# A decoder step on one core: first two blocks of B together, then dt with both weight parts side by side

## The chip, the cores and the metric

The kernel runs on one core of one Trainium2 chip. The metric is device time in microseconds (us) of one execution. Engines are named as in the profile: PE multiplies matrices (PEld loads its stationary operand), DVE, ACT and POOL work on vectors, SP issues the DMAs.

## The reference, cut to what matters

One layer of a hybrid decoder. 304 tokens (16 meta, 256 of a prompt, 32 of eight running sequences) of width 2048 are normalized by RMSNorm and multiplied by one input projection, whose columns are the gate and input of an RG-LRU group, and z, x, B, C and dt of a Mamba-2 group. Convolution, recurrences, an output projection and a squared-ReLU MLP follow. For the change only this part matters:

```python
def rmsnorm(x, g):
    y = xf * lax.rsqrt(jnp.mean(xf * xf, axis=-1, keepdims=True) + EPS)
    return (y * g.astype(jnp.float32)).astype(x.dtype)
...
proj = h @ w_in            # h = rmsnorm(x, g_mix)
gate_lru, x_lru, z, xbc_raw, dt_raw = proj[..., :o1], ...
dt = jax.nn.softplus(dt_raw.astype(jnp.float32) + dt_bias.astype(jnp.float32))
```

dt has only 32 columns (one for each head). B and C have 512 columns each, x and z 2048 each, the LRU part 4096.

## The kernel before, in words

**Layout and tiling.** Features lie on the 128 partitions, tokens on the free axis. x is 16 tiles of 128 x 304 (index k). A *block* is 128 output columns of a projection: 16 k-tiles, and for each three matmuls, since float32 is multiplied as two parts: hi is the value rounded to the type that PE multiplies at full speed (fp32r), lo is the rest; the three products are hi·hi, weight hi times activation lo, weight lo times activation hi. So a block is 48 matmuls of some 304 columns into one PSUM bank (`gemm`, L92). The kernel has dt and 72 blocks of the input projection, 32 of the output projection, 64 and 64 of the MLP: 233 blocks.

**Weights.** `prep` (L74) loads a block's 1 MB into a raw buffer (two of these), ACT writes hi (L87) and DVE lo = raw − hi (L88) in two halves of eight k-tiles. There are four buffers for hi halves and four for lo halves, which hold two blocks. For the first blocks the 1 MB comes in four DMAs of 256 KB (`cuts`), later in one. `run_blocks` (L128) prepares up to two blocks ahead of the one that multiplies.

**Start.** SP issues, in this order, the dt weights (256 KB), the parameters (173 KB), 16 tiles of x (152 KB each), four quarters each of the first two blocks of B, the constants (380 KB) and a convolution state (288 KB). ACT writes hi of g_mix·x (x0h, L214), DVE lo (x0l, L215). POOL squares x tiles 0 to 7 (L218) and adds them in a tree (L220). The dt weights are copied four times across the 128 columns (L204), so that dt comes out on all four groups of 32 partitions; POOL makes the lo part of their second half (L207). dt is the first block, then B0 to B3, C0 to C3 and x tiles X0 to X3 (list ph1, L617), all on the x that is not yet normalized (x0): the scale 1/rms of a token is multiplied in when the block leaves PSUM (`rsb`). From X4 on the blocks use the normalized x (xa).

**What sets the order.** Work beside the matmuls is given out by generators. `pump` (L115) takes the next step of the first generator; it is called three times within a block and once behind it. The first generator is `norm_x` (L223): its first step emits the squares of tiles 8 to 15 (ACT) and their sums (DVE), then come seven empty steps, then the matmul that sums over partitions (`ms_all`, L170, the eighth pump), the square root, the reciprocal (L178), and the work of blocks that had to wait for the scale (`held`); from then on it normalizes one x tile in three pumps (L237 to L247), which fills xa. When it is through, `tables` (L335) makes dt's softplus and tables, and the SSD cores follow. Within these bounds the framework orders the instructions of each engine by a simulated timeline, earlier emission first; weight splits have a raised priority (L86). Engines then take their queues in order.

**PSUM.** There are eight banks: three take turns for blocks (pool psg), five for the rest and for the first three blocks (L94). A block's bank is free when its post step has read it; for B, C and X0 to X3 that is `fill_ext` (L280), which needs `rsb` and one of three `ext` buffers. So a block can begin once the post step of the third block before it has read its bank.

## Time and profile before

| what | us |
| --- | --- |
| time, median of 3 runs (least, greatest) | 1631.81 (1631.64, 1633.52) |
| the profiled execution's own time | 1631.34 |
| its span in the profile | 1629.2 |
| PE, PEld busy | 1606.7, 1579.8 |
| DVE, ACT, POOL busy | 1058.2, 831.3, 254.1 |

A busy PE is one that has a matmul in its pipeline; consecutive matmuls overlap, so their cost is read from the distance of their starts and not from their durations. "x0h", "whi" and so on are the program's names of tiles; "s" and "g" are PSUM banks of the two pools; L58, L61, L69 and L101 are lines of helpers that all tensor operations, fused operations, activations and block matmuls share, so tiles and shapes tell them apart.

### The profile page before, as it was taken

How to read it: one execution, taken by the hardware profiler on the slowest of the kernel's cores; microseconds unless marked ns; L12 is line 12 of the kernel's file. 1: busy time of each engine (PE TensorE's matmuls, PEld its weight loads, DVE VectorE, ACT ScalarE, POOL GpSimd, SP SyncE). 2: the span in 40 equal slices, each digit the busy share in tenths (PEclk: the TensorE clock that was granted, in tenths of full speed). 3: DMA queues.
4: the chain of work that ended last, by engine and by line, in shares of the span. 5: the costliest groups of instructions: out<-in, count | busy, mean ns of one | idle time of the engine just before them, and what ended most of it. 6: DMA issues, size and time to landing. Idle time of an engine off the chain costs nothing.

```text
span 1629.2 us, 28889 instructions
## 1 busy us (share of the span) xinstructions
PE 1606.7 (99%) x11855; PEld 1579.8 (97%) x11855; DVE 1058.2 (65%) x1542; ACT 831.3 (51%) x1299; POOL 254.1 (16%) x311
## 2 busy tenths in 40 slices
PE   7999999999999999999999999999999999999997
PEld 6999989889999999999999999999999999999997
DVE  7999998989787878456565434544445555455554
ACT  5656677557777774344444334443334433344442
POOL 4554534432232310011220000000000000000000
PEclk9999999999999999999999999999999999999999
DMA  6454555554444446454454444544544545445442
GB/s 218 156 181 148 196 194 196 174 188 151 164 166 165 166 151 225 158 176 158 156 176 161 160 177 156 168 168 158 175 160 160 176 156 170 167 158 175 160 162 104
DMA packets 53988, 274.28 MB, mean 168 GB/s; under 512 B 5984, under 2 KB 12768, under 8 KB 24544
## 3 DMA queue, kind: packets, MB, share of 16 engines
q1 hardware_dynamic: 53856, 272.44, 49.2%
q8 instruction: 93, 1.52, 0.4%
q14 instruction: 39, 0.32, 0.1%
HBM read 259.99 MB, written 12.42 MB: 167 GB/s over the span
## 4 chain that ended last, share of the span: by engine, by line
PE 92%; DMA 3%; DVE 2%; ACT 1%; issue 1%; POOL 0%; SPq 0%; DVEq 0%; POOLq 0%; ACTq 0%
PE g L101 86%; DMA out_sssd<-h 1%; PE s L101 1%; PE s L762 1%; DMA wraw<-in_win 1%; PE s L438 1%; DMA h<-in_stssd 1%; ACT whi L69 0%; POOL h0l L58 0%; DVE z L58 0%; PE s L562 0%; DVE h L58 0%; PE s L436 0%; PE s L559 0%; PE s L448 0%
## 5 line engine op out<-in xcount | busy, mean ns | idle before, releaser
L58 DVE TENSOR_TENSOR wlo<-wraw,whi 128x1024 fp32r<-128x1024 f32 (+1 forms) x470 | 572.7, 1221 | 428.7 <-ACT whi L69 425.1
L69 ACT ACTIVATE whi<-wraw 128x1024 fp32r<-128x1024 f32 (+1 forms) x470 | 491.6, 1048 | 649.2 <-PE g L101 593.2
L101 PE MATMUL g<-mh,whi 128*128 128x288 f32 x1024 | 303.5, 296 | 0.0
L101 PE MATMUL g<-hh,whi 128*128 128x288 f32 x1024 | 303.4, 296 | 0.0
L101 PE MATMUL g<-hl,whi 128*128 128x288 f32 x1024 | 302.8, 296 | 0.0
L101 PE MATMUL g<-ml,whi 128*128 128x288 f32 x1024 | 302.5, 295 | 0.0
L101 PE MATMUL g<-hh,wlo 128*128 128x288 f32 x1024 | 301.7, 295 | 0.0
L101 PE MATMUL g<-mh,wlo 128*128 128x288 f32 x1024 | 301.6, 295 | 0.0
L101 PE MATMUL g<-xh,whi 128*128 128x288 f32 (+1 forms) x960 | 287.8, 300 | 0.4 <-DVE ext L287 0.4
L101 PE MATMUL g<-xl,whi 128*128 128x288 f32 (+1 forms) x960 | 287.7, 300 | 0.0
L101 PE MATMUL g<-xh,wlo 128*128 128x288 f32 (+1 forms) x960 | 286.8, 299 | 0.0
L101 PEld LDWEIGHTS g<-hh,wlo 128*128 128x128 f32 x1024 | 193.1, 189 | 0.0
L101 PEld LDWEIGHTS g<-mh,wlo 128*128 128x128 f32 x1024 | 193.1, 189 | 0.0
L101 PEld LDWEIGHTS g<-hl,whi 128*128 128x128 f32 x1024 | 192.9, 188 | 0.0
L101 PEld LDWEIGHTS g<-hh,whi 128*128 128x128 f32 x1024 | 192.8, 188 | 0.0
L101 PEld LDWEIGHTS g<-ml,whi 128*128 128x128 f32 x1024 | 192.4, 188 | 0.0
L101 PEld LDWEIGHTS g<-mh,whi 128*128 128x128 f32 x1024 | 192.2, 188 | 0.0
L101 PEld LDWEIGHTS g<-xh,whi 128*128 128x128 f32 x960 | 180.7, 188 | 3.5 <-issue 1.0
L101 PEld LDWEIGHTS g<-xh,wlo 128*128 128x128 f32 x960 | 180.9, 188 | 2.7 <-issue 1.2
L101 PEld LDWEIGHTS g<-xl,whi 128*128 128x128 f32 x960 | 180.7, 188 | 2.2 <-issue 0.7
L101 PE MATMUL g<-lh,whi 128*128 128x288 f32 x256 | 75.8, 296 | 0.0
L101 PE MATMUL g<-sh,whi 128*128 128x288 f32 x256 | 75.8, 296 | 0.0
(273 smaller groups left out, 2329.3 us busy)
## 6 DMA issues: line engine op xcount, KB each, us to landing
wraw<-in_win SPq DMA_DIRECT2D x69, 1024.0 KB, 5.0
wraw<-in_wup SPq DMA_DIRECT2D x64, 1024.0 KB, 4.9
wraw<-in_wdn SPq DMA_DIRECT2D x64, 1024.0 KB, 4.9
wraw<-in_wout SPq DMA_DIRECT2D x32, 1024.0 KB, 5.0
h<-in_stssd SPq DMA_DIRECT2D x32, 256.0 KB, 3.1
out_sssd<-h SPq DMA_DIRECT2D x32, 256.0 KB, 3.0
wraw<-in_win SPq DMA_DIRECT2D x12, 256.0 KB, 5.1
big<-in_x SPq DMA_DIRECT2D x16, 152.0 KB, 3.5
```

The costliest lines, as they stand in the source:

```text
L58: e.tensor_tensor(out, a, b, op=op)
L69: A.activation(out, in_, f, **kw)
L101: TE.matmul(o, a[:, k % 8, :], b[:, c0:c1], start=n == 0, stop=n == 3 * NK - 1)
L438: TE.matmul(po[0:66, :], cm[:, 66 * b:66 * b + 66], a[:], start=b == 0 and n == 0, stop=b == 7 and n == 1)
L762: TE.matmul(pr[:, :FL], w_[:, m, :], x_[:], start=n == 0, stop=n == 2)
```

## The change

Where the tiles of x are loaded, the quarters of the weights of B0 and B1 are loaded and split in between (`take_w`, `split_w`), through one raw buffer of two halves. `run_first` multiplies B0 and B1 in one loop over k, six matmuls for each k-tile, and behind it dt: hi and lo of the 32 dt columns lie side by side in one stationary operand of 66 columns (two are zero), so dt takes two matmuls for each k-tile, 32 in place of 48; its two halves come out on partitions 0 to 31 and 32 to 63. `tables` adds them and spreads them over 128 partitions with one float32 matmul of 304 columns by a selection matrix, a step later than before. Eleven small matmuls on constants run at the start, before any data is there. The dt weights are loaded behind x. All 16 squares of x are ACT's, all sums are DVE's; POOL has none of them, nor a weight split. Normalizing a tile takes two pumps in place of three. `run_first` has one pump, so `ms_all` is emitted at the third pump within B3, and the held blocks are dt, B0, B1 and B2.

```diff
@@ -187,44 +187,88 @@
     rsb = x0p.tile([P, T], F32, tag="rsb", bufs=1, name="rsb")
     sqx = x0p.tile([P, 8, T], F32, tag="sqx", bufs=1, name="sqx")
     sqa = sqx[:, 0, :]
+    bf = [sp.tile([P, T], F32, tag="bf", bufs=4, name=f"bf{g}") for g in range(4)]
+    cf = [sp.tile([P, T], F32, tag="cf", bufs=4, name=f"cf{g}") for g in range(4)]
     held, scaled = [], []
     xts, x0, xa = [], [], []
     warm = cst.tile([P, 1], F32, name="warm")
     act(warm[:], ones[:], AF.Exp)
-    rdt = x0p.tile([P, NK, 32], F32, tag="rdt", bufs=1, name="rdt")
-    SY.dma_start(rdt[:], I["wdt"])
+    wps = bank()
+    for _ in range(11):
+        TE.matmul(wps[:, 0:P], ones[:].to_broadcast([P, P]), ones[:].to_broadcast([P, P]), start=True, stop=True)
     SY.dma_start(par[:], I["par"])
-    parts = []
+    first = [[], []]
+    raw4 = wp.tile([P, NK, P], F32, tag="wraw", bufs=2, name=nm("wraw"))
+    def take_w(q):
+        s0 = 8 * (q % 2)
+        for n, ap in enumerate(win[0:2]):
+            SY.dma_start(raw4[:, s0 + 4 * n:s0 + 4 * n + 4, :], ap[:, 4 * q:4 * q + 4, :])
+    def split_w(q):
+        s0, m = 8 * (q % 2), 4 * (q % 2)
+        for n, f in enumerate(first):
+            if m == 0:
+                f.append([wp.tile([P, 8, P], F32R, tag=t, bufs=4, name=nm(t)) for t in ("whi", "wlo")])
+            r = raw4[:, s0 + 4 * n:s0 + 4 * n + 4, :]
+            wh, wl = [t[:, m:m + 4, :] for t in f[-1]]
+            act(wh, r, AF.Copy)
+            tt(V, wl, r, wh.bitcast(F32), SUB)
     for k in range(NK):
-        if k % 8 == 0:
-            parts.append([wp.tile([P, 8, P], F32R, tag=t, bufs=4, name=nm(t)) for t in ("whi", "wlo")])
-        if k % 4 == 0:
-            r = rdt[:, k:k + 4, None, :].to_broadcast([P, 4, 4, 32])
-            wh, wl = [t[:, k % 8:k % 8 + 4, :].rearrange("p k (c j) -> p k c j", j=32) for t in parts[-1]]
-            act(wh, r, AF.Copy)
-            tt(V if k < 8 else G, wl, r, wh.bitcast(F32), SUB)
         xt = bigt()
         SY.dma_start(xt[:], I["x"][:, k, :])
         xts.append(xt)
+        if k % 4 == 1:
+            take_w(k // 4)
         gm = par[:, C_GMIX + k:C_GMIX + k + 1]
         hi = x0p.tile([P, T], F32R, tag="xh", name=nm("x0h"))
         lo = x0p.tile([P, T], F32R, tag="xl", name=nm("x0l"))
         act(hi[:], xt[:], AF.Copy, scale=gm)
         stt(lo[:], xt[:], gm, hi[:].bitcast(F32), MUL, SUB)
         x0.append((hi, lo))
-        if k < 8:
-            tt(G, sqx[:, k, :], xt[:], xt[:], MUL)
-    for n in (4, 2, 1):
-        tt(G, sqx[:, 0:n, :], sqx[:, 0:n, :], sqx[:, n:2 * n, :], ADD)
-    ready[id(wdt)] = parts
+        if k % 4 == 1:
+            split_w(k // 4)
+    rdt = x0p.tile([P, NK, 32], F32, tag="rdt", bufs=1, name="rdt")
+    SY.dma_start(rdt[:], I["wdt"])
+    wd = x0p.tile([P, 64 * NK + 2], F32R, tag="wd", bufs=1, name="wd")
+    wd3 = wd[:, 0:64 * NK].rearrange("p (k j) -> p k j", j=64)
+    V.memset(wd[:, 64 * NK:].bitcast(F32), 0.0)
+    act(wd3[:, :, 0:32], rdt[:], AF.Copy)
+    tt(V, wd3[:, :, 32:64], rdt[:], wd3[:, :, 0:32].bitcast(F32), SUB)
+    def run_first(posts):
+        pss_ = [bank() for _ in range(3)]
+        for k in range(NK):
+            for f, ps in zip(first, pss_[1:]):
+                hi, lo = f[k // 8]
+                xh, xl = x0[k]
+                for n, (a, b) in enumerate(((hi, xh), (hi, xl), (lo, xh))):
+                    TE.matmul(ps[:, :T], a[:, k % 8, :], b[:], start=k == 0 and n == 0,
+                              stop=k == NK - 1 and n == 2)
+        for k in range(NK):
+            for n, b in enumerate(x0[k]):
+                TE.matmul(pss_[0][0:66, :T], wd[:, 64 * k:64 * k + 66], b[:],
+                          start=k == 0 and n == 0, stop=k == NK - 1 and n == 1)
+        blocks[0] += 3
+        done.extend(range(3))
+        for ps, post in zip(pss_, posts):
+            held.append(lambda post=post, ps=ps: post(ps))
+        pump()
     def norm_x():
-        for k in range(8, NK):
-            sq = sp.tile([P, EXT], F32, tag="th", bufs=2, name=nm("sq"))
-            act(sq[:, :T], xts[k][:], AF.Square)
-            tt(V, sqa, sqa, sq[:, :T], ADD)
+        for k in range(NK):
+            act(sqx[:, k, :] if k < 8 else (bf + cf)[k - 8][:], xts[k][:], AF.Square)
+        for k in range(8):
+            tt(V, sqx[:, k, :], sqx[:, k, :], (bf + cf)[k][:], ADD)
+        for n in (4, 2, 1):
+            tt(V, sqx[:, 0:n, :], sqx[:, 0:n, :], sqx[:, n:2 * n, :], ADD)
         for _ in range(7):
             yield
         ms = ms_all(sqa, T)
@@ -242,7 +286,6 @@
             act(hi[:], xts[k][:], AF.Copy)
             tt(V, lo[:], xts[k][:], hi[:].bitcast(F32), SUB)
             xa.append((hi, lo))
-            yield
             yield
             yield
@@ -302,8 +345,6 @@
         return flat[:, S0:EXT].rearrange("p (b s) -> p b s", s=7)[:, :, 0:4]
-    bf = [sp.tile([P, T], F32, tag="bf", bufs=4, name=f"bf{g}") for g in range(4)]
-    cf = [sp.tile([P, T], F32, tag="cf", bufs=4, name=f"cf{g}") for g in range(4)]
     xf = [None] * 16
     yt_ = [None] * 16
     ys_ = []
@@ -329,14 +370,22 @@
     def post_dt(ps):
         x0 = bigt()
-        tt(V, x0[:], ps[:, :T], rsb[:], MUL)
+        tt(V, x0[0:64, :], ps[0:64, :T], rsb[0:64, :], MUL)
         gens.append(tables(x0))
-    def tables(x0):
+    def tables(y0):
+        yield
+        px = bank()
+        s4 = sp.tile([64, 4, 32], F32, tag="dup", bufs=1, name="s4")
+        V.tensor_copy(s4[:], con[0:64, None, K_SEL:K_SEL + 32].to_broadcast([64, 4, 32]))
+        TE.matmul(px[:, :T], flat(s4), y0[0:64, :],
+                  start=True, stop=True)
+        x0 = bigt()
+        V.tensor_scalar(x0[:], px[:, :T], par[:, C_DTB:C_DTB + 1], None, op0=ADD)
         b1, b2, b3 = [bigt() for _ in range(3)]
         dt = sp.tile([P, EXT], F32, tag="cv", bufs=2, name="dt")[:, :T]
         th1, th2 = [sp.tile([P, EXT], F32, tag="th", bufs=2, name=nm("th"))[:, :T] for _ in range(2)]
-        V.tensor_scalar(x0[:], x0[:], par[:, C_DTB:C_DTB + 1], None, op0=ADD)
         softplus(dt, x0[:], (b1[:], th1, th2, b2[:], b3[:]))
         nega = cst.tile([P, 1], F32, name="nega")
         act(nega[:], par[:, C_AL:C_AL + 1], AF.Exp)
@@ -609,19 +658,17 @@
                 gens.append(ssd_core(o // 4))
         return f
-    for w in win[0:2]:
-        ready[id(w)] = prep(w, 4)
-        done.append(id(w))
     SY.dma_start(con[:], I["con"])
     SY.dma_start(stsc[:], I["stsc"])
-    ph1 = [(wdt, x0, 0, T, post_dt)]
+    ph1 = []
     for g in range(4):
         ph1.append((win[g], x0, 0, T, lambda ps, g=g: post_conv(ps, 16 + g, bf[g], rsb)))
     for g in range(4):
         ph1.append((win[4 + g], x0, 12, T, lambda ps, g=g: post_conv(ps, 20 + g, cf[g], rsb, 12)))
     for o in range(4):
         ph1.append((win[8 + o], x0, 0, T, post_x(o)))
-    run_blocks(ph1, win[12:14])
+    run_first([post_dt] + [b[4] for b in ph1[:2]])
+    run_blocks(ph1[2:], win[12:14])
     while len(xa) < NK:
         pump()
     x0_stack.close()
```

## Rows read from the trace of the kernel before

**Rows 1.** The page, busy time, share of the span and instructions of each engine.
```profile
PE 1606.7 (99%) x11855; PEld 1579.8 (97%) x11855; DVE 1058.2 (65%) x1542; ACT 831.3 (51%) x1299; POOL 254.1 (16%) x311
```

**Rows 2.** PE's waits, whole span: us in total, times, longest.
```profile
PE s L101 <- ACT x0h L69: 6.2, 1, 6.2
PE s L101 <- DVE x0l L61: 3.2, 5, 1.8
...
PE g L101 <- DVE ext L287: 0.4, 1, 0.4
```

**Rows 3.** Timeline of PE: start us, duration us, line, operation, count.
```profile
22.06 0.46 PE L101 MATMUL s<-x0h,wlo 128*128 128x304 f32 x1
...
23.33 0.46 PE L101 MATMUL s<-x0l,whi 128*128 128x304 f32 x1
...
24.79 0.30 PE L101 MATMUL s<-x0l,whi 128*128 128x304 f32 x1
...
25.90 0.30 PE L101 MATMUL s<-x0h,whi 128*128 128x304 f32 x1
...
30.92 0.30 PE L101 MATMUL g<-x0h,whi 128*128 128x304 f32 x1
...
37.35 0.68 PE L173 MATMUL s<-sqx,ones 128*128 128x304 f32 x2
...
38.00 0.30 PE L101 MATMUL s<-x0l,whi 128*128 128x304 f32 x1
...
104.08 0.30 PE L101 MATMUL g<-xh,whi 128*128 128x304 f32 x1
```

**Rows 4.** Windows, block matmuls: stretch, length, PE busy (count), granted clock, DMA share, GB/s.
```profile
6.19:20.88 14.69, 11.45 (x34) 1.00 0.92 306
20.88:23.58 2.70, 2.70 (x11) 1.00 0.00 0
```

**Rows 5.** Groups of 0 to 24 us: shapes, count, busy us, mean ns, idle before.
```profile
L61 DVE SCALAR_TENSOR_TENSOR x0l<-big,par,x0h 128x304 fp32r<-128x304 f32 x16 | 16.4, 1100 | 0.3 <-ACT x0h L69 0.3
...
L58 POOL TENSOR_TENSOR sqx<-big 128x304 f32<-128x304 f32 x8 | 6.8, 875 | 4.7 <-DMA big<-in_x 4.7
...
L58 POOL TENSOR_TENSOR sqx<-sqx 128x1216 f32<-128x1216 f32 x1 | 2.9, 2877 | 0.1
```

**Rows 6.** Tile x0l, DVE: duration ns least, median, greatest; first and last start.
```profile
L61 DVE SCALAR_TENSOR_TENSOR x0l<-big,par,x0h x16: 523/960/3032, 6.2 to 22.1; 128x304 fp32r<-128x304 f32 x16
```

**Rows 7.** Timeline of SP's queue: DMAs issued.
```profile
0.74 0.39 SPq L197 DMA_DIRECT2D rdt<-in_wdt  x1
...
1.65 7.54 SPq L209 DMA_DIRECT2D big<-in_x  x16
9.23 3.98 SPq L78 DMA_DIRECT2D wraw<-in_win  x8
```

**Rows 8.** Timelines of POOL and ACT: first reader of three loads, which waited for it.
```profile
5.18 1.44 POOL L58 TENSOR_TENSOR sqx<-big 128x304 f32<-128x304 f32 x2 [4.75 <-DMA big<-in_x]
...
21.16 1.07 POOL L291 COPY ext<-stsc 128x24 f32<-128x24 f32 x3 [0.67 <-DMA stsc<-in_stsc]
...
13.85 0.63 ACT L69 ACTIVATE whi<-wraw 128x512 fp32r<-128x512 f32 x1 [0.33 <-DMA wraw<-in_win]
```

**Rows 9.** Tile cm, PE: matmuls with 66 stationary columns, duration ns least, median, greatest.
```profile
L438 PE MATMUL s<-h0h,cm x8: 390/396/403, 159.7 to 184.3; 128*66 128x512 f32 x8
```

**Rows 10.** Timeline of DVE: weight splits, the scale, the last xl, a bank's release.
```profile
22.54 4.90 DVE L58 TENSOR_TENSOR wlo<-wraw,whi 128x512 fp32r<-128x512 f32 x8
...
38.60 2.05 DVE L178 RECIPROCAL rsb<-rsb 128x304 f32<-128x304 f32 x1 [1.11 <-ACT rsb L69]
...
115.77 0.47 DVE L58 TENSOR_TENSOR xl<-big,xh 128x304 fp32r<-128x304 f32 x1
...
124.38 0.28 DVE L287 COPY ext<-g 128x32 f32<-128x32 f32 x2
```

**Rows 11.** Windows: length, then busy (count) of PE, PEld, DVE, ACT, POOL.
```profile
40.70:116.20 75.50, 75.50 (x551) 75.50 (x550) 71.28 (x146) 44.99 (x68) 38.35 (x47) 1.00 0.49 166
```

**Rows 12.** Groups of DVE, 41 to 116 us: shapes, count, busy us, mean ns.
```profile
L58 DVE TENSOR_TENSOR wlo<-wraw,whi 128x1024 fp32r<-128x1024 f32 x23 | 27.9, 1218 | 3.9 <-ACT whi L69 3.8
```

## Prediction

> **What bounds the kernel now.** I read the busy shares first, then PE's waits, then the first 40 us engine by engine, then the stretch from 40 to 125 us. PE is busy for 99% of the span [rows 1], and of its waits only the two at the start are long: 6.2 us until the first x0h, and five waits of 3.2 us together for x0l [rows 2]. So the kernel is PE's stream of matmuls from end to end, and what can be won is at the start, or matmuls left out.
>
> How fast PE runs is read from the distance of starts. At 22 us five matmuls take 1.27 us, 0.254 each, which is 304 columns at 1.2 GHz; from 24.79 to 25.90 eight take 1.11 us, 0.139 each, which is the 2.4 GHz level with some 0.012 us on top [rows 3]. The granted clock reads 1.00 in both stretches [rows 4], so only the distances show the level. PE ran at the lower one all through the dt block: from 6.19 to 20.88 us it was busy for 11.45 of 14.69 us, in pieces, and stayed low; from 20.88 to 23.58 it never stopped, and then rose [rows 4].
>
> B1 starts at 30.92 us [rows 3], so dt and B0 took until then, and the three blocks end 48 x 0.139 = 6.67 us later, at **37.6 us** (the matmul for the mean square, which cuts in at 37.35, left out). At full pace 144 matmuls are 20.0 us: the start loses 17.6 us.
>
> Why dt was slow stands in the DVE rows. The 16 x0l took 16.4 us, 1.10 us each [rows 5], while the shortest took 0.523 and the longest 3.03 us [rows 6]. The longest is as long as POOL's 1216-element sum, 2.88 us [rows 5]; POOL was squaring and adding all this time. So DVE's late x0l held PE, and DVE came to the weights of B0 only at 22.54 us [rows 10], though their first quarter was there at 13.85 [rows 8].
>
> **The change, part by part.** *Loads.* The first x tile was there at 5.18 us with 581 KB issued (dt weights, parameters, x0), the convolution state at 21.16 with all 5577 KB [rows 8]: 4996 KB in 15.98 us, 313 KB/us. The first weight quarter (3117 KB) fits to 0.4 us [rows 8]. The queue starts at 0.74 as before [rows 7]; the 256 KB of dt no longer stand in front, so x0 lands at 5.18 − 0.82 = 4.36, and what lies n KB into the queue at 4.36 + (n − 325)/313. In the new order: first quarters of B0, B1 (733, 989 KB) 5.7, 6.5; x5 (1597) 8.4; second quarters (2109) 10.1; x9 (2717) 12.0; third (3229) 13.6; x13 (3837) 15.6; fourth (4093, 4349) 16.4, 17.2; x15 (4653) 18.2; dt weights (4909) 19.0; B2 (6601) 24.4. SP takes 7.54/16 = 0.47 us for an x tile and 3.98/8 = 0.50 for a quarter [rows 7], 12 us in all, so the transfers and not SP set the pace. The third quarter's DMA waits for the first one's split, which stands ahead of x10; that split is through by about 8 us, when SP gets there, and the data in front lands until 12.0, so nothing runs dry.
>
> *Splits.* For four k-tiles DVE has four x0l of 0.52 us and two weight splits of 0.61 (4.90/8, [rows 10]): 3.3 us, against 1120 KB or 3.6 us of loads. This holds if x0l takes its short duration; since POOL has no sum or square left, I take that one. If x0l kept its mean of 1.10 us, four k-tiles would take 5.6 us, and the loop would end some 8 us later.
>
> *The loop.* B0's first matmul can start at 5.7 + 0.63 for hi [rows 8], 6.3 us, as early as dt's did. Six matmuls at 0.139 are 0.83 us for a k-tile, 13.3 us for the loop; at 0.254 they would be 1.52 us, more than the 0.9 us in which the data for one k-tile arrives. So a slow PE falls behind the loads, runs without a stop, and by [rows 4] rises; a fast one is held by the loads. The last quarters give whi and wlo at 17.0 to 18.5 us, and four k-tiles from 17.7 are through at 21.1. Behind it dt has 32 matmuls of 304 columns. With 66 stationary columns a matmul of 512 columns takes 0.39 to 0.40 us [rows 9], no less than its columns need, so I take 0.139: 4.45 us. The three blocks end at **25.6 us**. Bounds: data at 18.2, then 1.05 us of split and one k-tile, loop 20.1, end 24.5; PE at 1.2 GHz for all 128 matmuls, 6.3 + 32.5 = 38.8. I stay near the first: the unbroken stream that brought the clock up is there by the second group of four at the latest. The eleven warm matmuls read a constant and are done before the data comes; I give them nothing, and at worst they keep PE some us past 6.3, which the loads hide.
>
> The Trainium skill, "TensorE: Matmul & The Clock Gate", section "Loop structure matters more than you think", speaks against a loop that waits for DMAs between its matmuls: PE goes cold there. By that rule the loop would never hold the upper level; the third rival below prices it from rows. The trace agrees as far as the dt block goes, which had gaps and stayed low [rows 4].
>
> So PE comes to B2 12.0 us earlier. 2.2 of it is 16 matmuls that no longer exist, the rest is the start.
>
> *What comes back.* (a) B2's 1 MB comes in one DMA, at 24.4 us. Two hi halves and two lo halves follow; the first lo, at 1.22 us [rows 12] behind about 1.1 of hi (an estimate, twice 512 elements' 0.63 less its fixed part), is there at 26.7. PE can run two matmuls from 25.6 and then waits: 0.9 us. Its hi and lo buffers are free by then, since k-tiles 0 to 7 are through at about 14. (b) The selection matmul: the mean-square matmul has the same form, and from its start at 37.35 to the second block matmul behind it at 38.00 are 0.65 us [rows 3], less one ordinary 0.14: +0.5 us. (c) Its extra step, the copy of s4 and the addition of the bias lie beside matmuls: nothing on the path, as tables begin near X4 in both kernels. (d) Sixteen squares are ACT's, some 7 us of it, and the sums move to DVE (8 tiles, then 1216, 608 and 304 elements; by 0.61 us for 512, some 5.5 us). They have from 20 to 37 us, where DVE has only the splits of B2 to C0 besides, about 7 us: nothing. If that cover were gone, the scale would be late one for one.
>
> (e) The scale. `ms_all` is emitted in B3 behind k-tile 11: 25.6 + 0.9 + 6.67 + 5.0 = 38.2 us, against 37.35 before. The reciprocal was through at 40.65 [rows 10]; now it is at about 41.5. So PE is 12 us ahead and everything that needs the scale is not. Before, from 40.7 to 116.2, where the last xl ends [rows 10], DVE was busy for 71.28 of 75.5 us [rows 11]; PE did not wait, since X4 from 104.08 on [rows 3] and X5 were interleaved over the tiles of xa that were there. So DVE is as tight as PE here. What does DVE save up to the last xl? 23 split halves lay in that stretch [rows 12]. Now PE, and with it the splits, is ahead: C0 and half of C1 are split before 41.5, three halves more than B3's first before, and X4 comes some 51 us after the scale in place of 63, 1.8 blocks or 3.6 halves fewer. Two pumps for each tile put the last xl ahead of X2's and X3's post work (about 2.4 us each, three times 0.55 and two reads) and of tables' first 4 us. 6.6 x 1.14 + 4.8 + 4 = 16 us less: last xl at about 41.5 + 75.5 − 16 = 101. PE starts X4 at 25.6 + 0.9 + (104.08 − 37.6) = 93.0, the last xl is 8 us behind; before it was 12.1. That is no worse, but the post work put off (9 us) comes later, and the bank that X7 needs was read at 124.38, with 0.4 us of waiting already [rows 2, 10]. I take 1.0 us of new waits here; bounds 0 and the 9 us.
>
> **Sum.** −12.0 + 0.9 + 0.5 + 1.0 = −9.6 us. The profiled execution took 1631.34 (span 1629.2, 2.1 around it), which gives 1621.7; the median is 0.47 above it, so **1622.2 us**.
>
> **Rivals.** *DVE takes half of it back.* If the 9 us put off fall due while PE is a whole 12 us ahead, PE waits for banks at X4 to X7: 5 us more than my 1.0 or so, **1627 us**. For it: the 94% of [rows 11]. Against: the xl arrive with no worse distance.
>
> *The clock stays low.* Waits for loads in every group keep PE at 0.254 us: the loop ends at 6.3 + 24.4 = 30.7, dt at 2.4 GHz at 35.1, at 1.2 GHz 38.8. Lead 2.5 us or −1.2, less 0.5: **1630 to 1633.5**. For it: [rows 4], first row. Against: at 0.254 there are no waits in the loop.
>
> *A bank is late, and the kernel slower.* After `run_first` PE has three banks for B2, B3 and C0; C1 needs B2's, whose post step waits for the scale. C0 ends at 25.6 + 0.9 + 13.3 + 0.5 + 6.4 = 46.7. With the scale at 41.5 the bank is read by about 44. From a scale later than 44 on, each us is PE's; slower than before from 54 to 55 on. DVE's sums queued behind splits that wait for loads could do this; one whole block's late sums plus the 2 us reciprocal would bring it to 57, **1634 us**. Against: 10 us of room on DVE.
>
> *It does more than I say*: waits (a) and (e) nil, **1620**.
>
> **How the numbers follow.** The forecast has 0.60 (its own range 1619.5 to 1624.5), DVE's rival 0.20, the clock 0.10, the bank 0.05, the better case 0.05. About 0.2%, 3.3 us, can be told from no change. Faster by more: all of the forecast and the better case, 0.18 of DVE's rival, 0.02 of the clock's: 0.85. Within: 0.02 + 0.05 + 0.02 = 0.09. Slower: 0.03 each of clock and bank, 0.06. The range is 1618.5 to 1628: it takes in DVE's rival and leaves the clock's and the bank's out.
>
> **What would show it.** x0l at about 0.52 us throughout; the dt matmuls behind the loop, ending near 25.6; matmul distances of 0.139 well before 15 us; `ms_all` near 38; X4's first matmul near 93; PE's waits for DVE between 40 and 125 us small. If X4 starts near 93 and the time is not below 1625, the lead was given back later, and I am wrong on (e); if the loop ends past 25, I am wrong on the clock or the loads.

## The result, and the profile after

The changed kernel takes **1641.91 us** (median of 4 runs, 1641.14 to 1645.73), the kernel before 1632.26 beside it (1631.64 to 1633.52): ratio 1.0065, 95% interval 1.0051 to 1.008. I had said 1622.2 and faster; it is 9.7 us slower. The profiled execution took 1641.28 us, its span is 1639.5.

Busy times of the page after, against [rows 1]:

```profile
PE 1613.4 (98%) x11863; PEld 1582.2 (97%) x11863; DVE 1052.0 (64%) x1544; ACT 828.9 (51%) x1300; POOL 210.8 (13%) x298
```

PE's waits after, against [rows 2] (us in total, times, longest). Those for x0h and x0l are gone; in their place stand 14 small ones, nine of them between 115 and 255 us, where the kernel before waited once, for 0.4 us. The largest groups:

```profile
PE g L101 <- DVE ext L330: 2.4, 2, 2.0
PE s L487 <- ACT h0h L69: 2.4, 2, 1.2
PE s L253 <- ACT whi L69: 2.1, 2, 1.8
PE g L101 <- DVE tz L61: 1.7, 1, 1.7
PE s L608 <- DVE em L58: 1.7, 1, 1.7
PE s L558 <- DVE xw L58: 1.2, 1, 1.2
```

**The opening works, but brings 8.0 us and not 12.0.** The 16 x0l take 0.53 us each, against 1.10 [rows 5, 6]; dt's 32 matmuls lie 0.14 us apart. But the loop ends at 25.1 us and not at 21.1. The first real matmul and the loop's two waits, dt's first and last matmul, and the mean square (PE's timeline after: start, us, ..., idle time before it):

```profile
7.73 0.41 PE L253 MATMUL s<-x0h,whi 128*128 128x304 f32 x1 [1.75 <-ACT whi L69]
...
20.45 0.41 PE L253 MATMUL s<-x0h,whi 128*128 128x304 f32 x1 [0.30 <-ACT whi L69]
...
22.19 0.41 PE L253 MATMUL s<-x0h,wlo 128*128 128x304 f32 x1 [0.68 <-DVE wlo L58]
...
25.09 0.33 PE L257 MATMUL s<-x0h,wd 128*66 128x304 f32 x1
...
29.41 0.30 PE L257 MATMUL s<-x0l,wd 128*66 128x304 f32 x1
...
41.28 0.67 PE L173 MATMUL s<-sqx,ones 128*128 128x304 f32 x2
```

The three blocks end at 29.55 us, against 37.6. Within the loop PE is held by the last quarter: its hi from 20.45 us on and its lo, which DVE begins only at 21.46. ACT's timeline shows where 2 of the missing 4 us are: the squares, which I had put between 20 and 37 us, stand between the x0h from 8.69 us on, 0.35 us each from start to start, and ACT has no pause until 22.9; the last quarter's hi, expected at 17 to 18.5, is made from 19.78 to 20.92:

```profile
8.25 0.53 ACT L69 ACTIVATE x0h<-big,par 128x304 fp32r<-128x304 f32 x1
8.69 0.44 ACT L69 ACTIVATE sqx<-big 128x304 f32<-128x304 f32 x1
9.04 0.53 ACT L69 ACTIVATE x0h<-big,par 128x304 fp32r<-128x304 f32 x1
...
19.78 1.14 ACT L69 ACTIVATE whi<-wraw 128x512 fp32r<-128x512 f32 x2
```

**The scale comes later than before.** The sum of the squares is ready at 32.2 us, but the matmul over it is given out at the eighth pump, and the first three blocks now have one pump in place of twelve: 41.28 us. The reciprocal and the last two xl, against [rows 10] (DVE's timeline after):

```profile
42.58 2.05 DVE L178 RECIPROCAL rsb<-rsb 128x304 f32<-128x304 f32 x1 [0.60 <-ACT rsb L69]
...
112.88 0.85 DVE L58 TENSOR_TENSOR xl<-big,xh 128x304 fp32r<-128x304 f32 x2
```

So PE leads by 8 us, and what hangs on 1/rms is 4.0 us late. The last xl is through at 113.7 us; I had said 101. It was 116.2 before. From 41 us on DVE is as busy as before (70.41 of 74.90 us from 41.3 to 116.2; [rows 11]).

**Where it is given back.** I compared the end of each block's matmuls in both traces. X3 ends 7.2 us ahead, and X4 starts at 96.9 us (104.08 before; I had said 93). X7 begins with a wait of 2.05 us for `ext`, which is the wait for a bank that I had priced at 1 us. Z2 still ends 10.0 ahead (230.1, 240.1). Then Z3 begins 11.4 behind, at 251.31 against 239.9, and some 10 us behind it stays to the end. In the hole stand rows of SSD core 1 alone (samples, heads, `em`, `hst`; the expectations below count 25 of them in the built order), with no block matmul between them, and PE goes from one to the next at the pace of what they wait for. Some of them (PE's timeline after):

```profile
232.66 0.45 PE L487 MATMUL s<-h0h,cm 128*66 128x512 f32 x1 [1.22 <-ACT h0h L69]
234.02 0.44 PE L487 MATMUL s<-h0l,cm 128*66 128x512 f32 x1 [0.90 <-POOL h0l L58]
235.66 2.05 PE L558 MATMUL s<-xw,bt 128*128 128x512 f32 x2 [1.20 <-DVE xw L58]
...
240.33 0.70 PE L608 MATMUL s<-em,xdt 128*64 128x128 f32 x4 [1.74 <-DVE em L58]
...
251.31 0.40 PE L101 MATMUL g<-xh,whi 128*128 128x288 f32 x1 [1.75 <-DVE tz L61]
```

The clock goes with it (windows after: span, us, busy us and count of PE, PEld, DVE, ACT, POOL, granted clock, DMA share, GB/s). From 228 to 242 us PE is busy for 8.5 of 14 us; from 234.6 us on it gets half the clock, 1.2 GHz, which slows what is left to do. Behind a stretch at the full level the clock is low once more, under block matmuls without a pause:

```profile
228.00:234.00 6.00, 3.45 (x19) 2.33 (x17) 6.00 (x8) 5.14 (x15) 2.00 (x2) 1.00 0.61 242
234.00:238.00 4.00, 2.78 (x5) 1.07 (x5) 3.51 (x6) 3.80 (x8) 0.07 (x1) 0.57 0.49 155
238.00:242.00 4.00, 2.26 (x11) 0.97 (x10) 4.00 (x6) 0.00 (x0) 1.20 (x1) 0.50 0.90 284
242.00:248.00 6.00, 6.00 (x29) 3.52 (x27) 3.38 (x9) 1.04 (x2) 1.27 (x1) 0.50 0.83 275
...
234.60:248.20 13.60, 10.80 (x40) 5.59 (x40) 10.48 (x18) 4.34 (x9) 2.54 (x2) 0.50 0.75 244
251.60:255.00 3.40, 3.40 (x16) 3.40 (x16) 3.40 (x10) 0.70 (x2) 1.55 (x2) 0.50 0.22 82
```

Why Z3 can't begin: it needs the bank of Z0, whose post step needs `tz`. That tile takes turns with the convolutions' `cv`, of which there are two, and X14's last operation reads one of them only at 245.69 (DVE's timeline after); it stands behind the first `big<-ea,s` of core 1 in DVE's queue.

```profile
245.35 0.42 DVE L58 TENSOR_TENSOR big<-ea,s 128x256 f32<-128x256 f32 x1 [1.52 <-PE s L611]
245.69 0.54 DVE L61 SCALAR_TENSOR_TENSOR big<-th,cv 128x272 f32<-128x272 f32 x2
...
250.82 0.44 DVE L61 SCALAR_TENSOR_TENSOR tz<-tz,g 128x288 f32<-128x288 f32 x1
```

The same two operations before:

```profile
218.08 0.53 DVE L61 SCALAR_TENSOR_TENSOR big<-th,cv 128x272 f32<-128x272 f32 x2
...
224.04 0.44 DVE L61 SCALAR_TENSOR_TENSOR tz<-tz,g 128x288 f32<-128x288 f32 x1
```

And the whole stretch from 130 to 375 us, before and after (windows): before, PE was busy for 244.1 of 245 us **and** DVE for 225.2, 92%, and the granted clock read 1.00; after, it is 0.97.

```profile
130.00:375.00 245.00, 244.10 (x1758) 221.42 (x1756) 225.23 (x384) 163.96 (x351) 95.90 (x104) 1.00 0.54 180
```

```profile
130.00:375.00 245.00, 236.00 (x1633) 207.88 (x1632) 217.80 (x370) 154.33 (x342) 80.24 (x104) 0.97 0.51 172
```

**What the loss is made of.** From the end of X3 to the end of the same block near 640 us PE has the same 3857 matmul instructions in both kernels and takes 17.2 us longer (windows, before and after):

```profile
104.24:637.48 533.24, 531.18 (x3857) 507.70 (x3857) 467.29 (x804) 367.38 (x681) 171.87 (x224) 1.00 0.52 174
```

```profile
97.07:647.53 550.46, 539.41 (x3857) 510.83 (x3857) 472.40 (x816) 367.68 (x685) 151.25 (x228) 0.98 0.50 169
```

PE stands idle 9.0 us longer (11.05 against 2.06) and is busy 8.2 us longer. The clock makes up most of the second part: PE is busy for 14.2 us at half the clock (the two rows above), and half of that, 7.1 us, is my estimate of what it costs. The kernel before has no such stretch between 24 and 1620 us.

### The profile page after: what moved, and what is told of

It is laid out like the page before. It is cut to its first block, busy times and chain, and to the rows that moved or that the text cites. A ratio compares the mean times of both kernels' runs of the same rounds, so it can differ in the third digit from the quotient of the medians.

```text
span 1639.5 us, 28894 instructions
## 1 busy us (share of the span) xinstructions
PE 1613.4 (98%) x11863; PEld 1582.2 (97%) x11863; DVE 1052.0 (64%) x1544; ACT 828.9 (51%) x1300; POOL 210.8 (13%) x298
## 4 chain that ended last, share of the span: by engine, by line
PE 92%; DVE 4%; DMA 2%; issue 1%; ACT 1%; SPq 0%; DVEq 0%; ACTq 0%
PE g L101 87%; DVE wlo L58 1%; PE s L809 1%; DMA out_sssd<-h 1%; DVE cv L61 1%; PE s L487 1%; DVE h L58 1%; PE s L608 1%; PE s L611 0%; DVE big L61 0%; PE s L485 0%; DMA con<-in_con 0%; DMA h<-in_stssd 0%; PE s L558 0%; DVE z L58 0%
```

## The experiments

Three theories were tested. *Order*: the change gives the cores out two steps earlier against the blocks, so their rows fall into one run ahead of Z3. *Ring*: one tile more is taken from the ring of 24. *VectorE* (at first called work): DVE with the cores' chain sets the pace, and a lead of PE alone can't be kept. The table has all kernels. "Lead" is how much earlier than in the kernel before X3 ends, and the block that ends there near 640 us; "core 0, 3" is the start of DVE's first `em` product of the first and the last core; "lost" is the difference of the two leads.

| kernel | lead X3 | core 0 | core 3 | lead 640 | lost | median, ratio to before (95%) |
| --- | --- | --- | --- | --- | --- | --- |
| before | 0 | 177.2 | 339.9 | 0 | 0 | |
| after | 7.2 | 177.4 | 346.5 | −10.0 | 17.2 | 1641.9, 1.0051 to 1.0080 |
| e1 | 6.8 | 178.2 | 346.7 | −6.7 | 13.5 | 1640.0, 1.0034 to 1.0067 |
| e2 | 7.3 | 175.5 | 339.8 | −5.7 | 13.0 | 1637.8, 1.0023 to 1.0047 |
| e4 | 4.1 | 180.7 | 351.0 | −16.5 | 20.6 | 1647.2, 1.0069 to 1.0102 |
| r4 | 6.3 | 178.4 | 347.9 | −10.8 | 17.1 | 1641.7, 1.0044 to 1.0075 |
| h1 | 7.4 | 176.2 | 342.3 | −6.1 | 13.5 | 1636.5, 1.0010 to 1.0036 |
| h7 | 7.8 | 174.0 | 343.5 | −2.3 | 10.1 | 1637.9, 1.0016 to 1.0043 |
| d1 | 6.2 | 177.0 | 338.5 | −4.2 | 10.4 | 1637.8, 1.0022 to 1.0045 |
| b1 | 0.0 | 167.3 | 336.5 | −12.5 | 12.5 | 1644.4, 1.0058 to 1.0088 |
| w8 | 5.2 | 188.5 | 349.4 | −7.4 | 12.6 | 1638.3, 1.0023 to 1.0053 |
| w9 | 7.7 | 188.2 | 352.6 | −14.1 | 21.8 | 1646.2, 1.0073 to 1.0107 |
| w12 | 7.4 | 190.0 | 355.1 | −16.2 | 23.6 | 1642.1, 1.0050 to 1.0090 |
| e3 | 6.6 | 188.6 | 356.1 | −15.9 | 22.5 | 1644.9, 1.0065 to 1.0095 |
| g2 | −1.4 | 170.5 | 332.5 | −5.6 | 4.2 | 1635.6, 1.0011 to 1.0030 |
| g1 | 6.1 | 175.8 | 334.9 | −1.0 | 7.1 | 1634.7, 1.0005 to 1.0023 |
| g3 | 7.5 | 170.4 | 332.5 | 1.7 | 5.8 | 1628.4, 0.9967 to 0.9986 |
| q5 | 8.1 | 174.6 | 345.4 | −4.7 | 12.8 | 1635.9, 1.0011 to 1.0030 |
| w3 | 5.0 | 174.6 | 337.5 | −1.7 | 6.7 | 1635.4, 1.0012 to 1.0030 |
| v3 | 6.1 | 177.7 | 344.4 | −10.2 | 16.3 | 1643.8, 1.0059 to 1.0100 |

The leads are of one profiled execution each, the medians of 4 to 10 runs. Those executions lie up to 5 us off the medians (h7 4.4 below, w12 5.3 above), so differences of a few us in the leads carry nothing.

What the loss is made of is the same in all 18: PE's added idle time between the same two points, and half of its busy time at half the clock there, together come within 3 us of "lost" (an estimate, as there). The clock's part is 1.6 to 7.7 us. So what is lost is, nearly all of it, PE's idle time and a clock that the kernel before keeps up here; what makes PE wait is the question of the experiments.

**e1, two empty steps more** at the head of `tables`.

```diff
         yield
+        yield
+        yield
         px = bank()
```

> The changed kernel with two more empty steps ahead of the dt tables, so that the step generators stand two steps further back against the blocks of X, about where they stood in the kernel before. Order theory (the result tiles of one ring are handed out in the order in which their first writes stand in the program; two steps further ahead put the first y tile of SSD core 1 ahead of the result of X14, so X14's last operation waits for core 1, with it the buffer that Z0's tanh product uses, with it the PSUM bank for Z3): X14's result is early again and X15's still late, so the hole of 21.5 us ahead of Z3 goes and a smaller one comes ahead of Z4: 1630 to 1640. Ring theory (one tile more in the ring of 24 is the cause): 1641 to 1643, as the changed kernel. Work theory (the SSD core chain is simply later than PE wants it, wherever it stands): 1640 to 1643, the hole moved by a block with its whole size.

The hole moved to Z4, as order says, and is half as long (241.2 to 252.1 us), but the time fell by 2 us only. 1640.0 lies on the border of the order and the work theory's ranges and decides nothing between them.

**e2, no tile more,** in `tables`.

```diff
-        x0 = bigt()
+        x0 = y0
```

> The changed kernel with the sum of dt and its bias written back into the tile that the product by 1/rms had, so that the ring of 24 tiles gives out as many tiles as before the change. Order theory: the hole ahead of Z3 stays, 1640 to 1643. Ring theory: the hole goes, 1622 to 1628. Work theory: 1640 to 1643.

The hole stayed (235.2 to 249.3 us): the ring's count does not make it. But 4 us came back, which no theory had.

**e4, squares behind the loads.**

```diff
+    zb = cst.tile([P, 1], F32, name="zb")
+    V.tensor_scalar(zb[:], wd[:, 64 * NK - 1:64 * NK].bitcast(F32), 0.0, None, op0=MUL)
...
-            act(sqx[:, k, :] if k < 8 else (bf + cf)[k - 8][:], xts[k][:], AF.Square)
+            act(sqx[:, k, :] if k < 8 else (bf + cf)[k - 8][:], xts[k][:], AF.Square, bias=zb[:])
```

> The changed kernel with all 16 squares of x made to wait until the dt weights are split (a bias of zero computed from them), so that they no longer stand between the first parts of x on ScalarE. If ScalarE was what stretched the opening (25.1 us instead of my 21.1): the two blocks end at 21 to 22.5, dt at 25.5 to 27, and the opening gains 2.5 to 4 us more. What that does at the end: the hole ahead of Z3 keeps its place in the order, and its end hangs on VectorE's and the loads' chain of core 1; if that chain follows the start, 1637.5 to 1639.5, if it does not, 1640 to 1643. If ScalarE was not the cause, the loop ends at 25 as it is.

The loop ends at 23.0 us, 2.1 earlier: the share of the squares on ACT, and of their sums on DVE, in the miss. PE has no wait in the loop then, and needs 15.2 us from 7.78 us on in place of 13.3; the rest is the loop's slow start, most of it a stretch at 1.2 GHz (8.86 to 11.14 us). But the squares, now from 21.2 to 28.3 us, hold up the hi halves of B2 on ACT, PE waits, and X3's lead is 3.1 us smaller. The scale is 3 us later, and everything behind it: 5 us slower. The squares have no free place on ACT.

**r4, early touch.** When X12's result tile is taken, those of X13 to X15 are taken too, by a write of one column on POOL:

```diff
-            xf[o] = bigt()
+            for q in range(12, 16) if o == 12 else (o,):
+                if xf[q] is None:
+                    xf[q] = bigt()
+                    if q > o:
+                        G.memset(xf[q][:, 0:1], 0.0)
```

> The changed kernel in which the result tiles of X13, X14 and X15 are taken from the ring when X12's are, by a write of one column on GpSimd (the column is overwritten later): nothing but the order in which the ring gives out its tiles is changed. Order theory: X14's last operation no longer stands behind core 1's y on VectorE, Z0's bank comes free before PE wants Z3, the hole of 21.5 us goes, with remains of a few us where single steps of core 1 still stand between Z blocks: 1624 to 1631. Ring theory: 1640 to 1643. Work theory (core 1's chain is late in itself): the hole moves to Z4 or Z5, 1637 to 1643.

Half of the order theory holds: `tz` of Z0 now runs at 235.80 (250.82 after), and Z3 begins at 236.35 without a wait for it and ends 6.5 us ahead of the kernel before. So the order in which ring tiles are first written does hold X14's operation behind core 1. The other half falls: the 17 us are lost all the same, at Z4, Z5 and Z9. Removing this hole gained nothing. 1641.7, with the loss moved on to Z4 and behind, is what the work theory had said.

**b1, one edit alone in the kernel before:** two steps instead of three for each scaled tile of x.

```diff
             xa.append((hi, lo))
             yield
             yield
-            yield
```

> The kernel before with one edit of the change alone: two steps for each scaled tile of x instead of three, so that the SSD cores are given out 16 steps earlier against the blocks. VectorE theory: VectorE's work and the time of 1/rms are as before, so the time is within 4 us of before, 1630 to 1637. Order theory: the place of the cores against the X blocks is what costs, and this moves it further than the change did: over 1640.

The fewer steps alone cost 12 us: the order expectation, and 7 us above VectorE's range. There is no lead here to give back, DVE's work is the same, the last xl comes 22 us earlier (93.77 us), and the cores are 10 us *earlier*. From 129 to 139 us PE is busy throughout at a granted clock of 0.51, which is 5 of the 12.5 us. Rows of the tables and of core 0 now stand in one run ahead of X7, which begins at 136.55 instead of 124.62 (PE's timeline of b1, first rows and the end of the run):

```profile
125.14 0.34 PE L361 MATMUL s<-con,big 64*128 64x64 f32 x2 [1.00 <-DVE big L354]
126.56 0.27 PE L361 MATMUL s<-con,t1d 64*128 64x64 f32 x1 [1.08 <-DVE t1d L327]
128.88 0.76 PE L369 MATMUL s<-tok,con 128*128 128x32 f32 x4 [2.05 <-DVE tok L363]
...
136.55 0.60 PE L101 MATMUL g<-xh,whi 128*128 128x304 f32 x1
```

**e3, that edit undone** in the changed kernel.

```diff
             xa.append((hi, lo))
             yield
             yield
+            yield
```

> The changed kernel with one part undone: three steps for each scaled tile of x, as before, instead of two. By the built order the 25 rows ahead of Z3 become 1, and 23 stand ahead of Z4. Order theory: the hole moves by a block and is about as large, 1634 to 1641. A theory that the fewer steps are the cause as such (they alone cost the kernel before 12 us): 1622 to 1630. VectorE theory: 1638 to 1642.

Slower still, and above the range of every theory: with the three blocks now one, the cores come later than before (188.6), and a hole of 12 us stands ahead of Z4. So the fewer steps are not by themselves the fault here.

**h1, scale early,** with five `yield` more in `tables`. **h7:** h1, e2 and r4 together. **d1:** two of the four taps left out for X4 to X11.

```diff
-        for _ in range(7):
+        for _ in range(2):
             yield
         ms = ms_all(sqa, T)
```

```diff
-    def conv(out, e, w, b):
+    def conv(out, e, w, b, taps=4):
         act(out, e[:, 0:FL], AF.Identity, bias=b, scale=w(0))
-        for k in range(1, 4):
+        for k in range(1, taps):
             stt(out, e[:, k:k + FL], w(k), out, MUL, ADD)
...
-        conv(cv[:, :FL], e, lambda k: hw[:, 24 * k + t:24 * k + t + 1], hw[:, 96 + t:97 + t])
+        conv(cv[:, :FL], e, lambda k: hw[:, 24 * k + t:24 * k + t + 1], hw[:, 96 + t:97 + t],
+             2 if 4 <= t < 12 else 4)
```

> The changed kernel with five of the seven empty steps that hold the mean of the squares back put behind it instead (ahead of the dt tables), so that 1/rms and what it scales come five steps, some 8 us, earlier, and the SSD cores stand at the same steps as before the edit. VectorE theory (from 40 us on VectorE sets the pace; the change gave TensorE 7 us at the start but put 1/rms 4 us later, so that the SSD cores' chain had no lead, and TensorE's was given back with more in holes): reciprocal of rsb at 33 to 36 instead of 42.6, the first product of core 0 with its mask (177.4) 4 to 8 us earlier, the end 4 to 8 us earlier: 1633 to 1638. Order theory (one place in the emission order makes the hole; the order here still has it, with 29 rows ahead of Z3): the lead at 100 us is larger or the same, the hole larger, 1639 to 1644.

> h1 with both other edits: no tile more in the ring of 24, and the result tiles of X13 to X15 taken from the ring when X12's are. VectorE theory: core 0's product with its mask 6 to 10 us earlier than in the changed kernel, and the holes shorter by as much: 1626 to 1634, about the kernel before or a little better. Order theory: the holes are split into 3, 8 and 14 rows ahead of Z3, Z4 and Z5: as with the early touch alone, 1638 to 1643.

> The changed kernel that leaves out two of the four taps in the convolutions of X4 to X11 (its output is not the reference's): 16 operations of 0.61 us, 9.8 us, less on VectorE between 100 and 230 us, all of TensorE's work as it is. VectorE theory: the holes between 110 and 360 us shrink by some 10 us, 1630 to 1634. Order theory (21 rows of core 1 still stand ahead of Z3): the hole stays within 3 us of 21.5, 1638 to 1642.

In h1 the reciprocal came at 37.45 us, 5.1 earlier, and the time fell by 5.4 us, inside VectorE's range. But VectorE's chain does not show: core 0 came only 1.2 us earlier (176.2), where 4 to 8 had been said. And the last xl was there before X4's first matmul (DVE's timeline of h1):

```profile
95.66 0.47 DVE L58 TENSOR_TENSOR xl<-big,xh 128x304 fp32r<-128x304 f32 x1
```

With neither the scale nor the xl late, 13.5 us were lost all the same. h7 and d1, where DVE has 16 operations less (its busy time fell by 6.8 us), are 4 us faster than the changed kernel, both 4 us above VectorE's ranges and just below order's. None of the three reached before.

**w8, w9, w12: empty steps chosen so that runs vanish.** `range(5)`, and 8, 9 or 12 more `yield` in `tables`; w12 with e2 and r4.

> The changed kernel with nothing but its empty steps altered: five instead of seven ahead of the mean of the squares, eight more ahead of the dt tables. In TensorE's queue no run of more than two rows of side work then stands between two blocks from C to Z15 (25 stand ahead of Z3 in the changed kernel). Order theory: the hole goes, what is left of the opening's 7 us stays: 1622 to 1628. VectorE theory: 1/rms comes 3 us earlier, the work is the same, the hole is paid elsewhere: 1635 to 1640.

> The same with one empty step more (nine). By the built order four runs of 4, 9, 14 and 4 rows of side work then stand ahead of Z1, Z3, Z5 and Z6. Order theory: 8 to 15 us slower than with eight, 1632 to 1640, and the lead over the kernel before falls at just these blocks. VectorE theory: within 1 us of the one with eight.

> Five empty steps ahead of the mean, twelve more ahead of the dt tables, no tile more in the ring of 24, and the result tiles of X13 to X15 taken early: no run of side work between blocks at all. Order theory: as with eight, 1620 to 1628. VectorE theory: 1634 to 1639; besides, with the cores four steps later than with eight, the last core may end behind the Z blocks and be waited for there, some 3 us.

One empty step between w8 and w9 is 8 us, where VectorE had said at most 1, so order does cost, and nearly as much as the change itself. But w8 and w12, which have no runs, are not fast and lie 10 and 14 us above order's ranges: runs of rows are not the whole. In w12 PE kept 12 us of lead up to Z2 and 8 to Z14, and then the second block behind Z15 stood still until Z14's post step had read its bank. The two steps before it need the last core's outputs, which DVE had at 375.3 us; from there the step's tanh came on ACT at 383.25 and its operation on DVE, behind three reciprocals, at 388.67 (PE's timeline of w12, the block's first two matmuls):

```profile
389.17 0.62 PE L101 MATMUL g<-xh,whi 128*128 128x304 f32 x1 [12.37 <-DVE tz L61]
389.59 0.46 PE L101 MATMUL g<-xl,whi 128*128 128x304 f32 x1
```

**g2, g1, g3: VectorE relieved.** Three of four taps of X4 to X15 left out, in the kernel before (g2), after (g1), and in h7 (g3). By the profile DVE's busy time fell by 17 to 18 us (16.8, 17.1, 18.2), not 22.

> Control: the kernel before, which leaves out three of the four taps in the convolutions of X4 to X15 (its output is not the reference's): 36 operations of 0.61 us, 22 us, less on VectorE between 105 and 250 us. Its TensorE was never idle between 130 and 300 us. VectorE theory: nothing to gain, TensorE is the bound there: within 3 us of the kernel before, 1629 to 1634. A theory that VectorE's work counts one for one in either kernel: 1610 to 1622.

> The changed kernel with the same 22 us left out on VectorE; 23 rows of side work still stand ahead of Z3. VectorE theory: the opening's 7 us come through in full or nearly, 1624 to 1630, that is 5 us or more faster than the kernel before with the same relief less what the run ahead of Z3 still costs. Accidental stalls by order: the run of 23 rows costs what it did, 1636 to 1642.

> The changed kernel with 1/rms five steps earlier, no tile more in the ring, the result tiles of X13 to X15 taken early, and the same 22 us left out on VectorE; no run of side work between blocks. VectorE theory: 1622 to 1626, the whole lead of 7 to 8 us kept over the kernel before. Accidental stalls: no run, so 1622 to 1626 too; it is g1 and the control that tell the two apart, this one shows what is to be had at most.

The same relief makes the changed kernel 7 us faster and h7 9.5, and the kernel before 3 us *slower*: PE had nothing to gain there from room on DVE, and 4.2 us were lost with no lead. With room on DVE the changed kernel is within 2.5 us of before, and with both edits 3.9 us faster (0.9977): the only one of 18 that was, and it leaves work out. Like against like, all three with the relief, g1 is 0.9 us and g3 7.2 us faster than g2. VectorE named the direction of g1 and g3, but g1 is 5 us above its range and g3 2 us; g2 is 2 us above its own.

**q5, w3, v3: versions that leave out nothing.** q5 is h7 with every third second half of `wlo` in X and Z on POOL; w3 has `range(3)` and r4; v3 is w3 with q5's edit.

```diff
-                    tt(V, wl, r, wh.bitcast(F32), SUB)
+                    tt(G if h == 1 and 14 <= len(done) < 36 and len(done) % 3 == 1 else V, wl, r, wh.bitcast(F32), SUB)
```

> A version that leaves out nothing: 1/rms five steps earlier, no tile more, the result tiles of X13 to X15 taken early, and in the blocks of X and Z every third second half of the weights' low part computed on GpSimd instead of VectorE (7 or 8 operations of 1.24 us, some 9 us less on VectorE). VectorE theory: 1628 to 1634, 4 to 9 us better than the same without (1637.9), unless GpSimd slows VectorE's operations beside it (in the kernel before a split of x took 0.96 us and more beside GpSimd's squares instead of 0.52), then 1634 to 1640.

> Leaves out nothing: the changed kernel with three instead of seven empty steps ahead of the mean of the squares (1/rms and the SSD cores come four steps earlier) and the result tiles of X13 to X15 taken early; no run of more than four rows of side work between blocks. Two conditions theory: last core's product with its mask at 335 to 341 us instead of 346.5, the end with it: 1626 to 1633, at least as fast as the kernel before. If each order simply has its own stalls: anywhere from 1634 to 1645, as the others.

> The same, and every third second half of the weights' low part in the blocks of X and Z on GpSimd, some 9 us less on VectorE. Two conditions theory: 1624 to 1632. Own stalls: 1634 to 1642.

w3 met both conditions that its expectation names (core 3 at 337.5, no run of more than four rows) and is, with q5 and h1, the best that leaves nothing out, 1635.4, yet slower than before by 3 us and above their range: the two conditions do not suffice. POOL takes 2.40 us for a half that takes DVE 1.23; with the order that the edit brings it gave h7 2 us and cost w3 8.

## Why the prediction was wrong

Of the 19.6 us between the forecast and the profiled execution, 3.4 lie ahead of X4 (a lead of 7.2 there, where 12.0 − 0.9 − 0.5 had been said) and 16.2 behind it.

*The opening, right in kind.* x0l at 0.52 and dt at 4.45 us came as said. The loop's end was 4.0 us off. One step that failed is (d), which put the squares and sums at "nothing": the squares are given out as soon as their tiles are there, ahead of work that PE waits for; e4 measures 2.1 us for them. (c) has the same fault in small: the copy for the selection matmul, which I had near X4, stands at 20.93 us with a sum ahead of the last quarter's lo. The other 1.9 us are the loop's slow start, mostly a stretch at 1.2 GHz (below), as e4 shows. The first matmul came at 7.73 instead of 6.3, since the first quarter of B0 landed at about 7.05 and not at 5.7. That the wait (a), forecast at 0.9, did not come is luck: B2's first lo was ready at about 27.5 us, behind the 25.6 that I had for dt's end, and only the late loop hid it.

*The scale.* 38.2 was forecast for `ms_all`, 41.28 came: the blocks' end is 4.0 us later than forecast, less the wait (a), since the matmul hangs on pumps of the blocks and not on the sum, ready at 32.2.

*Step (e) is the one that decided.* It took 1.0 us, at most 9, of new waits, and looked no further than X7. X4 to X7 cost 2.05 us. But the stretch in which PE and DVE are both nearly full goes on to 375 us, and between X3 and 640 us 17.2 us were lost: 9.0 of waiting and about 7 of lower clock. Its sum was wrong too, and not what decided: I had DVE 16 us quicker from the scale to the last xl (101 us), it was 6 (113.7); in b1 and h1 the last xl came at 94 and 96 us, and 12.5 and 13.5 us were lost. My bound was the 9 us of post work put off, a sum of work. It had no term for the order of the rows: in the kernel before, side rows and blocks interleave so that PE hardly stands, and b1 shows that one empty step per tile, with nothing else, takes 12.5 us of that away. Nor had it one for the clock behind a wait. I had counted fewer steps as a gain (the last xl earlier) and did not ask which rows then meet.

*What is shown and what is not.* Shown: the opening's lead of 7 us exists; it is lost between X4 and the end of Z, as idle time of PE and lower clock; order alone, with DVE's work the same, can cost 8 us (w8, w9) and 12 (b1); earlier scale, less DVE work, and other orders each give back 2 to 7 us. Not shown: one cause of the waits in the changed kernel. The first core's `em` had no lead at all (177.4 against 177.2), but that the late scale made it so is not shown: h1 has the scale 5.1 us earlier than the changed kernel, and `em` only 1.2. Order as a single place fell with r4 and w12, the ring with e2, VectorE alone with b1 and w9, the two conditions with w3. What fits all 18 is weaker: the order is fixed when the kernel is built, from that of before PE waits least, and each other order that was tried loses 4 to 24 us between X3 and 640 us. The four that leave DVE work out lose 4 to 10, and the ones with core 3 past 349 lose most, w8 excepted. That another order of the changed kernel keeps the 7 us is possible; none was found.

*Rivals.* The first (DVE takes half back) looked for 5 us more at X4 to X7, where 2.05 came; more than the whole lead was lost, most of it behind. The clock's rival, the second of the list (the prediction calls it the third), was wrong in its place: the opening rose to the upper level, and the clock fell in the hole at 234. The changed kernel's loop kept the upper level from 12.8 us on through waits of 0.30 and 0.68 us. That is not so in all runs with this opening: in w8 a wait of 1.31 us, and in w3 one of 0.98, stood ahead of a stretch at half the clock from 23 to 27 us (window of w8: span, us, ..., granted clock, DMA share, GB/s), while in g1 the clock stayed up behind 0.98:

```profile
23.00:27.00 4.00, 3.47 (x14) 3.47 (x15) 4.00 (x8) 1.80 (x5) 3.95 (x1) 0.59 0.80 260
```

The rule that the prediction weighed (the Trainium skill, "TensorE: Matmul & The Clock Gate", "Loop structure matters more than you think") speaks of a long wait before every matmul; no loop here had that, so it was not tested. The bank's rival did not come: PE has no wait for a bank between 30 and 100 us. Of the loads, the prediction's check on the first weight quarter is 0.6 us off, not 0.4, which changes nothing.

## What to carry to other kernels

Here two engines were both over 90% busy for hundreds of microseconds, and time won ahead of that stretch was not kept: ask what the change does to the order of the rows in it, and to the start of the second engine (here the scale, later), and not only when the bound engine arrives. A kernel whose side work is given out step by step is a fitted order; count for each edit by how many steps it moves every generator against the blocks, and look for runs of side rows ahead of a block, since in such a run PE goes at the pace of what each row waits for, and here at half the clock too. Before a change to the front, try the same shift of steps in the old kernel: b1 would have shown that two pumps for each tile are no gain.

## What was not expected of the hardware

The warm matmuls (22 rows, 0.92 to 5.99 us) did not carry PE through the opening. Distances were 0.14 us from 8.64 to 9.20 and then 0.25 (1.2 GHz for 304 columns) from 9.36 to 12.40, while PE multiplied without a stop; ahead of it lay the wait of 1.75 us. From 12.8 on they were 0.14 again. In kernels with the same opening, e4 aside, the loop's last matmul began between 24.8 and 27.8 us; the two latest, w3 and w8, are those with the second stretch at half the clock.

In w12, behind one wait of 12.37 us, PE had distances of 0.25 for 304 columns from 389.59 to 393.64 us: this wait cost once more after its end.
